# Results of six experts stored as long rows, with the tokens laid out to match

## The chip, the cores and the metric

The kernel runs on one core of a Trainium2 chip. The metric is device time in microseconds of one execution. Below, PE is TensorE (matrix products), DVE is VectorE, ACT is ScalarE, POOL is GpSimd and SP is SyncE; the last two mostly issue DMAs here.

## The reference

Eight experts each apply a two-layer network to their own 256 tokens: a product with w1, a bias, a ReLU, a product with w2 and a second bias.

```python
n_experts, capacity, hidden, expert_hidden = 8, 256, 512, 2048
# x [8, 256, 512], w1 [8, 512, 2048], w2 [8, 2048, 512], b1 [8, 2048], b2 [8, 512], all float32

def reference(x, w1, w2, b1, b2):
    h = np.matmul(x, w1) + b1[:, np.newaxis, :]
    h = np.maximum(h, 0)
    return (np.matmul(h, w2) + b2[:, np.newaxis, :]).astype(np.float32)
```

The weights are 67 MB in float32, x and the result 4.2 MB each.

## The kernel before

Weights are loaded by DMAs from GpSimd that turn float32 into float16 on the way. Each of the two weight pools has three buffers. Names: P = 128 partitions, nTB = 2 blocks of 128 tokens in an expert, nKC = 4 chunks of the hidden size, nJ = 16 chunks of the expert's hidden size, B = 32, LAG = 3.

The tokens come first. x of experts 0 and 1 is loaded as float32 by SyncE and cast by VectorE, two tokens to a partition; experts 2 and 3 share one load, four tokens to a partition; experts 4 to 7 share another, eight to a partition. The first product needs x with the hidden size on the partitions, so VectorE transposes blocks of 32 by 32. The order in which tokens stand in `xT` is free: whatever it is, the result comes out in that order. The code picks it so that partition p of the result's block tb holds token 2p + tb.

```python
    def transposes(e):
        t, p0, R = x16[e]              # R tokens to a partition
        n = R // nTB                   # 1, 2 or 4
        xT[e] = xT_pool.tile([P, nKC, T], fp16, tag="xT", name="xT")      # two buffers
        for g in range(T // R // B):
            src = t[p0 + B * g : p0 + B * (g + 1)]
            for b in range(nB):
                block = src[:, :, b * (H // nB) : (b + 1) * (H // nB)].rearrange(
                    "p (n tb) (i kc) -> p tb kc n i", tb=nTB, kc=nKC)
                out = xT[e][b * B : (b + 1) * B].rearrange(
                    "p kc (tb g i n) -> p tb g kc n i", tb=nTB, i=B, n=n)
                if n == 1:
                    nc.vector.transpose(out=out[:, :, g, :, 0, :], in_=block[:, :, :, 0, :])
                    continue
                for tb in range(nTB):
                    nc.vector.transpose(out=out[:, tb, g], in_=block[:, tb])
```

The first product adds b1 in the ReLU of ScalarE. b1 is brought on to the partitions by four transposes (`b1T`) on VectorE; in the order of the instructions they stand after the 16 transposes of expert 0 and the first seven of expert 1.

```python
    def first_product(e):
        for j in range(nJ):
            ph = psum_h.tile([P, T], fp32, ...)                           # three buffers
            for kc in range(nKC):
                matmul(out=ph, lhsT=w1_sb[e][...j...], rhs=xT[e][:, kc, :], ...)
            nc.scalar.activation(out=hT[e][:, j, :], in_=ph, func=Relu, bias=b1T[...], scale=1.0)
            if j == nJ // 2 and e + 1 < E:
                transposes(e + 1)
```

The second product leaves two blocks in PSUM, `po[0]` and `po[1]`. VectorE and ScalarE copy one each to SBUF, and the result is stored in rows of two tokens (4 KB). The stores of experts 0 to 5 are held back until every weight load is issued.

```python
    LATE = range(E - 2)
    PARTS = {E - 2: ((0, 25, False), (25, 121, True), (121, 128, False))}

    def flush(e):
        dst, src = pending.pop(e)
        ordered(nc.gpsimd.dma_start(out=dst, in_=src))

    def store(e, po):
        out_sb = out_pool.tile([P, nTB, H], fp32, tag="out", name="out")
        nc.vector.tensor_copy(out=out_sb[:, 0, :], in_=po[0])
        nc.scalar.copy(out=out_sb[:, 1, :], in_=po[1])
        dst = out[e].rearrange("(p tb) h -> p tb h", tb=nTB)
        if e in LATE:
            pending[e] = (dst, out_sb)
            return
        for p0, p1, scalar in PARTS.get(e, ((0, P, False),)):
            (nc.scalar if scalar else nc.sync).dma_start(out=dst[p0:p1], in_=out_sb[p0:p1])
    # ... (cut)
    ring.append((E + LAG - 3, load_w2, (E - 1, ((0, nJ // 2), (nJ // 2, nJ)))))
    for e in LATE:
        ring.append((e + LAG + 1, flush, (e,)))

    for s in range(E + LAG):
        while ring and ring[0][0] <= s:          # in the order of the list
            _, put, args = ring.pop(0)
            put(*args)
        if s < E:
            first_product(s)
        if s >= LAG:
            second_product(s - LAG)
```

Of the kernel before, what the change touches and what calls it, by code (L numbers as in the profile page):

```python
# [10 lines left out]
def kernel(  # L11
# [9 lines left out]
    nc = tc.nc  # L21
    fp32 = mybir.dt.float32
    fp16 = mybir.dt.float16
    E, T, H = x.shape
    M = w1.shape[2]
    P = 128
    nTB = T // P
    nKC = H // P
    nJ = M // P
    B = 32  # L30
    nB = P // B
    LAG = 3

    LATE = range(E - 2)


    PARTS = {E - 2: ((0, 25, False), (25, 121, True), (121, 128, False))}
# [3 lines left out]
    def ordered(ins):  # L43
        return tc.keep_in_program_order(ins)
# [4 lines left out]
    x_pool = ctx.enter_context(tc.tile_pool(name="xp", bufs=1))  # L49
    xT_pool = ctx.enter_context(tc.tile_pool(name="xTp", bufs=2))  # L50
    hT_pool = ctx.enter_context(tc.tile_pool(name="hT", bufs=LAG + 1))
    out_pool = ctx.enter_context(tc.tile_pool(name="outp", bufs=E))
    psum_h = ctx.enter_context(tc.tile_pool(name="psum_h", bufs=3, space=bass.MemoryType.PSUM))
    psum_o = ctx.enter_context(tc.tile_pool(name="psum_o", bufs=2, space=bass.MemoryType.PSUM))

# [6 lines left out]
    xT = [None] * E  # L62
    w1_sb = [None] * E
    w2_sb = [None] * E
    hT = [None] * E
    pending = {}

    def load_x(first, n):

        R = n * T // P  # L70
        t = x_pool.tile([P, R, H], fp16, tag=f"x{first}", name=f"x{first}")
        ordered(nc.gpsimd.dma_start(  # L72
            out=t, in_=x[first : first + n].rearrange("e (p r) h -> (e p) r h", r=R)
        ))
        for i in range(n):
            x16[first + i] = (t, i * (P // n), R)
# [13 lines left out]
    def transposes(e):  # L90


        t, p0, R = x16[e]
        n = R // nTB
        xT[e] = xT_pool.tile([P, nKC, T], fp16, tag="xT", name="xT")
        for g in range(T // R // B):
            src = t[p0 + B * g : p0 + B * (g + 1)]
            for b in range(nB):
                block = src[:, :, b * (H // nB) : (b + 1) * (H // nB)].rearrange(
                    "p (n tb) (i kc) -> p tb kc n i", tb=nTB, kc=nKC)  # L100
                out = xT[e][b * B : (b + 1) * B].rearrange(
                    "p kc (tb g i n) -> p tb g kc n i", tb=nTB, i=B, n=n)
                if n == 1:
                    nc.vector.transpose(out=out[:, :, g, :, 0, :], in_=block[:, :, :, 0, :])  # L104
                    continue
                for tb in range(nTB):
                    nc.vector.transpose(out=out[:, tb, g], in_=block[:, tb])  # L107

    def first_product(e):
        hT[e] = hT_pool.tile([P, nJ, T], fp16, tag="hT", name="hT")  # L110
        for j in range(nJ):
            bias_at = j * B + e * nB + nB - 1
            ph = psum_h.tile([P, T], fp32, tag="ph", name="ph")
            for kc in range(nKC):
                ordered(nc.tensor.matmul(  # L115
                    out=ph,
                    lhsT=w1_sb[e][:, kc, :].rearrange("p (q j) -> p q j", j=nJ)[:, :, j],
                    rhs=xT[e][:, kc, :],
                    start=(kc == 0),
                    stop=(kc == nKC - 1),  # L120
                ))
            nc.scalar.activation(  # L122
                out=hT[e][:, j, :],
                in_=ph,
                func=mybir.ActivationFunctionType.Relu,
                bias=b1T[:, bias_at : bias_at + 1],
                scale=1.0,
            )
            if j == nJ // 2 and e + 1 < E:
                transposes(e + 1)  # L130

    def flush(e):
        dst, src = pending.pop(e)
        ordered(nc.gpsimd.dma_start(out=dst, in_=src))  # L134

    def store(e, po):
        out_sb = out_pool.tile([P, nTB, H], fp32, tag="out", name="out")
        nc.vector.tensor_copy(out=out_sb[:, 0, :], in_=po[0])  # L138
        nc.scalar.copy(out=out_sb[:, 1, :], in_=po[1])  # L139
        dst = out[e].rearrange("(p tb) h -> p tb h", tb=nTB)  # L140
        if e in LATE:
            pending[e] = (dst, out_sb)
            return
        for p0, p1, scalar in PARTS.get(e, ((0, P, False),)):
            (nc.scalar if scalar else nc.sync).dma_start(out=dst[p0:p1], in_=out_sb[p0:p1])

    def second_product(e):
        po = []
        for tb in range(nTB):
            t = psum_o.tile([P, H], fp32, tag=f"po{tb}", name=f"po{tb}")  # L150
            po.append(t)
            ordered(nc.tensor.matmul(  # L152
                out=t, lhsT=ones1, rhs=b2_sb[0:1, e * H : (e + 1) * H], start=True, stop=False,
            ))
        half = nJ // 2 if e == E - 1 else nJ
        for lo in range(0, nJ, half):
            for tb in range(nTB):
                for j in range(lo, lo + half):
                    ordered(nc.tensor.matmul(  # L159
                        out=po[tb],  # L160
                        lhsT=hT[e][:, j, tb * P : (tb + 1) * P],
                        rhs=w2_sb[e][:, j, :],
                        start=False,
                        stop=(j == nJ - 1),
                    ))
        store(e, po)

    x32 = []
    for e in range(nXF32):
# [4 lines left out]
        out=b2_sb,  # L174
        in_=b2.rearrange("e h -> (e h)").rearrange("(o f) -> o f", o=1),
# [4 lines left out]
    for e in range(nXF32):  # L180
        t = x_pool.tile([P, nTB, H], fp16, tag=f"x{e}", name=f"x{e}")
        nc.vector.tensor_copy(out=t, in_=x32[e])  # L182
        x16[e] = (t, 0, nTB)
        if e == 0:
            transposes(e)


    for b in range(nB):
        nc.vector.transpose(  # L189
            out=b1T[b * B : (b + 1) * B, nB - 1 - b : nB - 1 - b + nJ * B],  # L190
            in_=b1_rows.rearrange("r (i j) -> r j i", j=nJ),
# [4 lines left out]
    ring = []  # L196
# [5 lines left out]
        if s >= LAG:  # L202
            ring.append((s - 2, load_w2, (s - LAG,)))
    ring.append((E + LAG - 3, load_w2, (E - 1, ((0, nJ // 2), (nJ // 2, nJ)))))
    for e in LATE:
        ring.append((e + LAG + 1, flush, (e,)))

    for s in range(E + LAG):
        while ring and ring[0][0] <= s:
# [37 lines left out]
```

## Time and profile before

| what | value |
|---|---|
| time, median of 3 runs | 182.44 us (182.09 to 182.93) |
| span of the profiled execution | 180.0 us |
| mean granted TensorE clock | 0.938 |
| DMA queue q0 (issued by GpSimd) | 96.5% of 16 engines' span |
| TensorE busy | 130.3 us (72%) |
| VectorE busy | 78.1 us (43%) |
| ScalarE busy | 62.5 us (35%) |

The span runs from the first to the last instruction of the program; the time is a little longer than that. The page's rows of digits cut the span into 40 slices of 4.5 us; a digit gives the busy share in tenths. GB/s counts the bytes of the packets as written, and a weight is written at half the bytes that it is read at. In lists of instructions, the number after x is a count, and what stands behind `<-` in brackets is what ended the engine's idle time.

### The profile page before, as it was taken

Reading aid. Unit: us, or ns where it says so; the run is one execution under the profiler, and the core shown is the slowest. Engines: PE = TensorE matmul, PEld = TensorE weight load, DVE = VectorE, ACT = ScalarE, POOL = GpSimd, SP = SyncE. Lnnn points to the kernel's source line nnn. Section 1 sums busy time; section 2 is a strip of 40 time slices with the busy share of each in tenths; the row PEclk is TensorE's granted clock in tenths of the full one; section 3 lists DMA queues with packets and bytes.
Section 4 is the critical chain, followed back from the end, with each engine's and each line's share of the span. In section 5 each row is a group of like instructions: output and inputs, shape, how many; then the busy total and the mean of one; then the engine's idle time right before and its main releaser. Section 6 shows DMA issues by size and latency. Waiting matters only on the chain.

```text
span 180.0 us, 1937 instructions
## 1 busy us (share of the span) xinstructions
PE 130.3 (72%) x784; PEld 87.4 (49%) x784; DVE 78.1 (43%) x111; ACT 62.5 (35%) x137; POOL 15.0 (8%) x31
## 2 busy tenths in 40 slices
PE   0006199999398950899769994959796899959960
PEld 0004079998286410794359543934395343324420
DVE  1999931988000099999990697000000010101010
ACT  0000558999177010491137403930186001100110
POOL 7100000220201010001100001000100008010000
PEclk9999999999879996599988999987999699999998
DMA  6999999998999999899999999999998999899996
GB/s 207 259 226 198 233 200 208 233 231 182 231 229 193 218 233 226 186 229 229 211 200 233 226 193 222 229 215 197 233 229 189 222 229 226 186 215 209 330 421 246
DMA packets 4260, 40.56 MB, mean 225 GB/s; under 512 B 508, under 2 KB 524, under 8 KB 1948
## 3 DMA queue, kind: packets, MB, share of 16 engines
q0 software_dynamic: 3664, 38.35, 96.5%
q1 hardware_dynamic: 476, 1.70, 2.6%
q10 hardware_dynamic: 112, 0.39, 0.5%
q8 instruction: 6, 0.10, 0.2%
q14 instruction: 2, 0.02, 0.0%
HBM read 71.39 MB, written 4.19 MB: 420 GB/s over the span
## 4 chain that ended last, share of the span: by engine, by line
DMA 44%; PE 30%; another core or an unknown queue 11%; DVE 9%; ACT 1%; issue 1%; POOL 0%; POOLq 0%; ACTq 0%
DMA w1sb<-in_w_dram 26%; PE ph L115 18%; DMA w2sb<-in_w_dram 17%; PE po L159 12%; DVE xT L104 6%; DVE b1T L189 2%; DMA x<-in_x_dram 2%; DVE x L182 1%; ACT L122 1%; PE po L152 1%; ACT out L139 0%; POOL w2sb L88 0%; ACT hT L122 0%; POOLq L88 0%
## 5 line engine op out<-in xcount | busy, mean ns | idle before, releaser
L115 PE MATMUL ph<-xT,w1sb 128*128 128x256 f16 x512 | 66.4, 298 | 36.2 <-DMA w1sb<-in_w_dram 24.9
L115 PEld LDWEIGHTS <-w1sb 128*128 128x128 f16 x512 | 60.9, 148 | 42.5 <-DMA w1sb<-in_w_dram 34.3
L107 DVE STREAM_TRANSPOSE xT<-x 32x256 f16<-32x256 f16 (+1 forms) x64 | 53.0, 888 | 31.9 <-DMA x<-in_x_dram 18.2
L159 PE MATMUL po<-w2sb,hT 128*128 128x512 f16 x256 | 59.7, 393 | 7.6 <-DMA w2sb<-in_w_dram 7.5
L122 ACT ACTIVATE hT<-ph,b1T 128x256 f16<-128x256 f32 x128 | 56.5, 474 | 24.6 <-PE ph L115 24.5
L159 PEld LDWEIGHTS <-hT 128*128 128x128 f16 x256 | 25.6, 100 | 41.6 <-issue 14.9
L138 DVE COPY out<-po 128x512 f32<-128x512 f32 x8 | 5.5, 692 | 58.3 <-PE po L159 58.2
L139 ACT COPY out<-po 128x512 f32<-128x512 f32 x8 | 4.7, 586 | 67.3 <-PE po L159 67.3
L104 DVE STREAM_TRANSPOSE xT<-x 32x256 f16<-32x256 f16 x32 | 13.9, 436 | 0.5
L88 POOL DMA_DIRECT2D w2sb<-in_w_dram x9 | 4.8, 532 | 73.3 <-PE po L159 73.3
L80 POOL DMA_DIRECT2D w1sb<-in_w_dram x8 | 4.9, 609 | 64.7 <-PE ph L115 63.9
L122 ACT ACT_TABLE_LOAD x1 | 1.3, 1283 | 20.2 <-DVE b1T L189 20.2
L152 PE MATMUL po<-b_sb,ones 1*128 1x512 f16 x16 | 4.8, 379 | 0.0
L189 DVE STREAM_TRANSPOSE b1T<-b_rows 32x512 f32<-32x512 f32 x4 | 4.1, 1037 | 0.1
L134 POOL DMA_DIRECT2D out_dram<-out x6 | 3.2, 536 | 7.2 <-DMA w2sb<-in_w_dram 7.2
L182 DVE CAST x<-x 128x1024 f16<-128x1024 f32 x2 | 1.4, 693 | 3.2 <-DMA x<-in_x_dram 3.2
L152 PEld LDWEIGHTS <-ones 1*128 1x128 f16 x16 | 0.9, 92 | 2.1 <-issue 2.1
L72 POOL DMA_DIRECT2D x<-in_x_dram x2 | 1.1, 554 | 0.0
L178 DVE MEMSET ones<- 1x128 f16 x1 | 0.2, 165 | 0.8 <-PEq L231 0.8
L177 POOL DMA_DIRECT2D b_rows<-in_b_dram x1 | 0.5, 515 | 0.0
L173 POOL DMA_DIRECT2D b_sb<-in_b_dram x1 | 0.5, 511 | 0.0
L231 POOL MEMSET const-float32-0.0<- 128x1 f32 x1 | 0.1, 99 | 0.2 <-issue 0.2
(3 smaller groups left out, 0.3 us busy)
## 6 DMA issues: line engine op xcount, KB each, us to landing
w1sb<-in_w_dram POOLq DMA_DIRECT2D x8, 2048.0 KB, 33.6
w2sb<-in_w_dram POOLq DMA_DIRECT2D x7, 2048.0 KB, 43.2
out_dram<-out POOLq DMA_DIRECT2D x6, 512.0 KB, 22.7
w2sb<-in_w_dram POOLq DMA_DIRECT2D x2, 1024.0 KB, 17.4
x<-in_x_dram SPq DMA_DIRECT2D x2, 512.0 KB, 3.8
x<-in_x_dram POOLq DMA_DIRECT2D x1, 1024.0 KB, 30.3
x<-in_x_dram POOLq DMA_DIRECT2D x1, 512.0 KB, 24.0
out_dram<-out SPq DMA_DIRECT2D x1, 512.0 KB, 4.4
```

The costliest lines, as they stand in the source:

```text
L80: ordered(nc.gpsimd.dma_start(out=w1_sb[e], in_=w1[e].rearrange("(p kc) m -> p kc m", kc=nKC)))
L88: ordered(nc.gpsimd.dma_start(out=w2_sb[e][:, lo:hi], in_=src[:, lo:hi]))
L104: nc.vector.transpose(out=out[:, :, g, :, 0, :], in_=block[:, :, :, 0, :])
L107: nc.vector.transpose(out=out[:, tb, g], in_=block[:, tb])
L115: ordered(nc.tensor.matmul(out=ph, lhsT=w1_sb[e][:, kc, :].rearrange("p (q j) -> p q j", j=nJ)[:, :, j], rhs=xT[e][:, kc, :], start=(kc == 0),
L122: nc.scalar.activation(out=hT[e][:, j, :], in_=ph, func=mybir.ActivationFunctionType.Relu, bias=b1T[:, bias_at : bias_at + 1], scale=1.0,)
L134: ordered(nc.gpsimd.dma_start(out=dst, in_=src))
L138: nc.vector.tensor_copy(out=out_sb[:, 0, :], in_=po[0])
L139: nc.scalar.copy(out=out_sb[:, 1, :], in_=po[1])
L152: ordered(nc.tensor.matmul(out=t, lhsT=ones1, rhs=b2_sb[0:1, e * H : (e + 1) * H], start=True, stop=False,))
L159: ordered(nc.tensor.matmul(out=po[tb], lhsT=hT[e][:, j, tb * P : (tb + 1) * P], rhs=w2_sb[e][:, j, :], start=False, stop=(j == nJ - 1),))
L189: nc.vector.transpose(out=b1T[b * B : (b + 1) * B, nB - 1 - b : nB - 1 - b + nJ * B], in_=b1_rows.rearrange("r (i j) -> r j i", j=nJ),)
```

## The change

The results of experts 0 to 5 no longer take one tile each. Experts 0 to 3 share a tile of 128 partitions, experts 4 and 5 one of 64: 32 partitions for an expert, and eight consecutive tokens (16 KB) on each. Each tile is stored by one DMA, so that a row of the store is 16 KB long and not 4 KB, and two DMAs take the place of six.

For this, token 8q + 2k + tb has to come out on partition 32k + q of the result's block tb. So the transposes write their columns in another order, and each block of the result is copied in four pieces of 32 partitions to the place it has in the shared tile. Where a block of x holds tokens of several of these quarters (f of them: 4 for experts 0 and 1, 2 for experts 2 and 3, 1 for 4 and 5) the order needs one dimension more, and the transposes of experts 0 and 1 come in twice as many instructions of half the size. Experts 6 and 7 stay as they were.

```diff
-    LATE = range(E - 2)
+    GROUPS = {0: 4, 4: 2}
+    SPLIT = 4
...
+    group_pool = ctx.enter_context(tc.tile_pool(name="groups", bufs=1))
-    out_pool = ctx.enter_context(tc.tile_pool(name="outp", bufs=E))
+    out_pool = ctx.enter_context(tc.tile_pool(name="outp", bufs=2))
...
         n = R // nTB
+        split = SPLIT if e in group_of else 1
+        f = 1 if split == 1 else split // n
+        to = ("p kc (tb g i f n) -> p tb g kc n i f" if split == 1
+              else "p kc (tb f n g i) -> p tb g kc n i f")
...
-                    "p (n tb) (i kc) -> p tb kc n i", tb=nTB, kc=nKC)
-                out = xT[e][b * B : (b + 1) * B].rearrange(
-                    "p kc (tb g i n) -> p tb g kc n i", tb=nTB, i=B, n=n)
-                if n == 1:
-                    nc.vector.transpose(out=out[:, :, g, :, 0, :], in_=block[:, :, :, 0, :])
+                    "p (n tb) (i f kc) -> p tb kc n i f", tb=nTB, kc=nKC, f=f)
+                out = xT[e][b * B : (b + 1) * B].rearrange(to, tb=nTB, i=B // f, f=f, n=n)
+                if n == 1 and f == 1:
+                    nc.vector.transpose(out=out[:, :, g, :, 0, :, 0], in_=block[:, :, :, 0, :, 0])
                     continue
...
-        out_sb = out_pool.tile([P, nTB, H], fp32, tag="out", name="out")
-        nc.vector.tensor_copy(out=out_sb[:, 0, :], in_=po[0])
-        nc.scalar.copy(out=out_sb[:, 1, :], in_=po[1])
-        dst = out[e].rearrange("(p tb) h -> p tb h", tb=nTB)
-        if e in LATE:
-            pending[e] = (dst, out_sb)
+        if e in group_of:
+            first, n = group_of[e]
+            split, rows = SPLIT, P // SPLIT
+            if e == first:
+                results[e] = group_pool.tile(
+                    [n * rows, split * nTB, H], fp32, tag=f"out{e}", name=f"out{e}")
+        else:
+            first, n, split, rows = e, 1, 1, P
+            results[e] = out_pool.tile([P, nTB, H], fp32, tag="out", name="out")
+        out_sb = results[first]
+        at = (e - first) * rows
+        for k in range(split):
+            part = slice(k * rows, (k + 1) * rows)
+            nc.vector.tensor_copy(out=out_sb[at : at + rows, k * nTB, :], in_=po[0][part])
+            nc.scalar.copy(out=out_sb[at : at + rows, k * nTB + 1, :], in_=po[1][part])
+        dst = out[first : first + n].rearrange("e (p r) h -> (e p) r h", r=split * nTB)
+        if e in group_of:
+            if e == first + n - 1:
+                pending[first] = (dst, out_sb)
             return
...
-    for e in LATE:
-        ring.append((e + LAG + 1, flush, (e,)))
+    for first, n in GROUPS.items():
+        ring.append((first + n + LAG, flush, (first,)))
```

More of the change, by code (lines that the diff above doesn't have):

```diff
@@ L66 @@
     pending = {}
+    results = {}
+    group_of = {first + i: (first, n) for first, n in GROUPS.items() for i in range(n)}
     def load_x(first, n):
@@ L130, in first_product, with flush @@
                 transposes(e + 1)
-    def flush(e):
-        dst, src = pending.pop(e)
+    def flush(first):
+        dst, src = pending.pop(first)
         ordered(nc.gpsimd.dma_start(out=dst, in_=src))
     def store(e, po):
-        out_sb = out_pool.tile([P, nTB, H], fp32, tag="out", name="out")
-        nc.vector.tensor_copy(out=out_sb[:, 0, :], in_=po[0])
-        nc.scalar.copy(out=out_sb[:, 1, :], in_=po[1])
-        dst = out[e].rearrange("(p tb) h -> p tb h", tb=nTB)
-        if e in LATE:
-            pending[e] = (dst, out_sb)
+        if e in group_of:
[17 more added lines that the diff above has]
+                pending[first] = (dst, out_sb)
             return
```

## The prediction

> **What bounds the kernel now.** I read the page's top first: the queue table and the three rows in tenths of the span.
>
> ```profile
> span 180.0 us, 1937 instructions
> PE 130.3 (72%) x784; PEld 87.4 (49%) x784; DVE 78.1 (43%) x111; ACT 62.5 (35%) x137; POOL 15.0 (8%) x31
> ...
> DMA  6999999998999999899999999999998999899996
> ...
> q0 software_dynamic: 3664, 38.35, 96.5%
> ...
> HBM read 71.39 MB, written 4.19 MB: 420 GB/s over the span
> ```
>
> No engine is busy for three quarters of the span, while GpSimd's DMA queue (q0) fills 96.5% of the 16 DMA engines' time. The DMA row has a low digit only in the first and the last slice. So the kernel is a stream of transfers, and two things can change its time: a stretch in which the stream has nothing to do, or packets that move their bytes at another rate.
>
> Next, the landings, asked of the weight loads one at a time. w1 of expert 2 is issued at 4.0 us and lands 33.1 us later, at 37.1; w1 of expert 3 is issued at 31.1 and lands 16.8 later, at 47.9; w2 of expert 0 at 58.1. One load of 4.19 MB takes 9.7 us wherever only weights flow, which is 432 GB/s. The important spot is the reload at 31 us, which the GpSimd timeline shows:
>
> ```profile
> 4.00 0.97 POOL L80 DMA_DIRECT2D w1sb<-in_w_dram  x1
> 31.08 0.53 POOL L80 DMA_DIRECT2D w1sb<-in_w_dram  x1 [26.11 <-PE ph L115]
> ```
>
> For 26 us nothing is issued; the queue lives on what was issued by 4 us, and that is used up at 37.1. The reload waits for TensorE's last read of expert 0's w1. It comes 6.0 us before the queue runs dry: that is all the slack there is. What TensorE waits for at this point is in the timeline of VectorE for the same stretch:
>
> ```profile
> 4.16 0.69 DVE L182 CAST x<-x 128x1024 f16<-128x1024 f32 x1 [3.17 <-DMA x<-in_x_dram]
> 4.88 7.18 DVE L104 STREAM_TRANSPOSE xT<-x 32x256 f16<-32x256 f16 x16
> 12.10 0.69 DVE L182 CAST x<-x 128x1024 f16<-128x1024 f32 x1
> 12.82 3.12 DVE L104 STREAM_TRANSPOSE xT<-x 32x256 f16<-32x256 f16 x7
> 15.96 4.19 DVE L189 STREAM_TRANSPOSE b1T<-b_rows 32x512 f32<-32x512 f32 x4
> ```
>
> VectorE works without a pause from 4.9 to 20.16 us, and only then is b1T there, for which the first ReLU waits ("ACT L122 <- DVE b1T L189: 20.2" in the view of waits). TensorE fills its three PSUM buffers and stands until 22.05. From there expert 0 takes to 30.8, and the reload follows at 31.1. So **any microsecond that VectorE loses before 20 us moves the reload**.
>
> Last, the end. The timeline shows TensorE without a gap from 159.39, when expert 6's w2 has landed, to 174.0; the last store is issued at 174.6 and lands 4.4 us later. The windows there have these columns: length, the five engines' busy time (count), clock, DMA share, GB/s.
>
> ```profile
> 150.00:152.00 2.00, 2.00 (x11) 0.87 (x9) 0.00 (x0) 0.00 (x0) 2.00 (x5) 1.00 1.19 254
> ...
> 170.00:172.00 2.00, 2.00 (x11) 0.93 (x10) 0.00 (x0) 0.00 (x0) 0.00 (x0) 1.00 1.01 414
> 172.00:174.00 2.00, 2.00 (x10) 0.68 (x7) 0.69 (x1) 0.00 (x0) 0.00 (x0) 1.00 1.05 426
> 174.00:176.00 2.00, 0.00 (x1) 0.00 (x0) 0.00 (x0) 0.59 (x1) 0.00 (x0) 1.00 1.01 412
> 176.00:178.00 2.00, 0.00 (x0) 0.00 (x0) 0.00 (x0) 0.00 (x0) 0.00 (x0) 1.00 0.96 391
> ```
>
> After 168 us only stores flow, and at full share. Weights count 4 bytes read and 2 written, so their 216 GB/s is 432 of reading; the stores' 410 or so is 95% of that already.
>
> [...]
> - [...] The second store after the change has 64 partitions. No run so far has such a transfer of size.
> - [...] of 32x512 transposes, those of experts 4 to 7 write every fourth element (8 bytes apart) and take 1328 ns, where the rate of the contiguous ones would give about 700.
> [...]
> - [...] between 170 and 172 us, q0 and the two other queues' packets alternate.
>
> **The change part by part.**
> 1. *The stores.* Removed: six stores of 128 rows of 4 KB, 48 packets per DMA engine. Added: two of 16 KB rows, 128 and 64 of them, 12 packets per engine. In the packet records a 4096-byte store packet takes 159 ns; a weight packet that reads 16 KB takes 625. If a 16 KB store packet takes as long as that, 4 x 159 = 636 becomes 625 or a little less: 12 x 11 = 0.13 us, with the marker packets (9 ns each) some 0.2 us. The bytes are the same and the engines were full. So the gain that the change is for is **0.2 us**, 0.1% of the time.
> 2. *Where they sit.* They still stand behind all loads in the queue, and start to move at about 168. Only the 64-partition store can differ[...]. I give that an even chance.
> 3. *Copies from PSUM.* Each expert's two copies become four on 32 partitions each. Duration follows the 512 elements per partition: VectorE 4 x 692 = 2.8 us, ScalarE 4 x 586 = 2.3 us per expert, +2.1 and +1.8. They fall at 81 to 160 us, where both engines are idle more than half the time and TensorE waits on weights. Worth 0 on the path.
> 4. *Transposes of experts 4 and 5.* Written contiguously now: 16 x (1328 - 700) = 10 us of VectorE saved, off the path. 0.
> 5. *Transposes of experts 0 and 1.* 16 instructions of 256 elements become 32 of 128 each, which write in the order "i f": neighbouring elements 64 bytes apart. This lies in the critical start: all 32 of expert 0 and 7 of expert 1 come before b1T. [...] With 13 ns between instructions, expert 0 takes 10.0, 15.1 or 24.4 us instead of 7.2; the seven take 2.2, 3.3 or 5.3 instead of 3.1. b1T is late by 1.9, 8.1 or 19.4 us.
> 6. *What that does to the stream.* The reload moves from 31.1 to 33.0, 39.2 or 50.5. Packets begin about 1.5 us after an issue (SyncE's first: issued 0.74, packet at 1.77[...]). The queue is dry at 37.1. Gap: none, 3.6 or 14.9 us. After it the queue is tens of microseconds deep (a load issued at 45.0 lands 46.5 later), so a gap is neither made up nor repeated. Experts 2 and 3, whose 16 transposes write 128 bytes apart, take 12 us each instead of 6.5 and delay TensorE, but weights wait for it there, not the other way round.
>
> Sum for the middle rate: 182.44 - 0.2 + 3.6 = 185.8[...].
>
> **Rivals.**
> - *The strided write is free, the stream never starves.* For it: elements 4 bytes apart cost nothing (448 ns against 436). Against: 8 bytes nearly double. Then -0.2 for the stores[...]: 182.2 to 184.3. 30%.
> - *Main line[...].* 185.8[...]. 45%.
> - [...] The gap is 15 us: 197 to 199; experts 2 and 3 then take 21 us each on VectorE, and the backlog is nearly used up later too. 25%.
> - *Long rows help more than packets tell.* TensorE ends at 174.0 and a lone 0.5 MB store needs some 3.4 us (the first x load took that), so the end cannot come before about 178.0: at most 1.2 us better, 181.2. Under 5%.
>
> **Range and chances.** The middle of these is at about 186.6. The low end, 181.9, is the free write with a small gain; the high end, 199[...]. More than 2% faster (below 178.8) is shut out by TensorE's end: 0.02. Above 186.1 fall the costly case (0.25) and somewhat over half of the middle one: 0.53 in all. The rest, 0.45, is within 2%.
>
> **What would show it.** The mean of the 32x128 transposes (298, 460 or 750 ns); the end of b1T (22, 28 or 39 us); the reload's issue (33, 39 or 50 us); a slice around 40 us where the DMA row falls under 8; w1 of expert 3 landing at 47.9 plus the gap. [...] I am wrong if b1T comes before 23 us, if the gap at 40 is there but made up later, or if the stores' last 10 us shrink by more than half a microsecond.

## The result, and the profile after

| | before | after |
|---|---|---|
| time, median | 182.26 us (182.04 to 182.93) | 202.67 us (202.14 to 203.35) |
| ratio | | 1.1117 (95% interval 1.1089 to 1.1145) |
| span of the profiled execution | 180.0 us | 200.4 us |
| mean granted TensorE clock | 0.938 | 0.932 |

The changed kernel takes 20.4 us more, above the stated range. The page's top shows where to look: q0 fell from 96.5% to 88.3% of the span, with the same 38.35 MB, and VectorE's busy time rose from 78 to 135 us. In the two rows of digits, each digit is one slice of 5 us.

```profile
span 200.4 us, 1997 instructions
...
DVE  2999999999999999999278069939913200450010
...
DMA  8999999208999999999999999999999997299994
...
q0 software_dynamic: 3024, 38.35, 88.3%
```

The transposes by shape, first before and then after, are those of experts 0 and 1, of 2 and 3, and of 4 to 7; behind the first bar stand their busy time in us and the mean of one in ns:

```profile
L104 DVE STREAM_TRANSPOSE xT<-x 32x256 f16<-32x256 f16 x32 | 13.9, 436 | 0.5
L107 DVE STREAM_TRANSPOSE xT<-x 32x256 f16<-32x256 f16 x32 | 12.8, 448 | 7.3 <-PE ph L115 7.1
L107 DVE STREAM_TRANSPOSE xT<-x 32x512 f16<-32x512 f16 x32 | 40.1, 1328 | 24.7 <-DMA x<-in_x_dram 18.2 <-PE ph L115 6.1
...
L114 DVE STREAM_TRANSPOSE xT<-x 32x128 f16<-32x128 f16 x64 | 41.2, 814 | 0.5
L114 DVE STREAM_TRANSPOSE xT<-x 32x256 f16<-32x256 f16 x32 | 39.9, 1431 | 0.2
L114 DVE STREAM_TRANSPOSE xT<-x 32x512 f16<-32x512 f16 x32 | 30.7, 1007 | 15.1 <-PE ph L122 14.8
```

The DMA row has two holes, near 40 us and near 170 us, and VectorE shows no pause from its first transpose to 95 us. VectorE's timeline, to set against the one of before:

```profile
4.80 20.67 DVE L114 STREAM_TRANSPOSE xT<-x 32x128 f16<-32x128 f16 x32
25.50 0.69 DVE L202 CAST x<-x 128x1024 f16<-128x1024 f32 x1
26.23 4.65 DVE L114 STREAM_TRANSPOSE xT<-x 32x128 f16<-32x128 f16 x7
30.89 4.13 DVE L209 STREAM_TRANSPOSE b1T<-b_rows 32x512 f32<-32x512 f32 x4
34.95 61.63 DVE L114 STREAM_TRANSPOSE xT<-x 32x128 f16<-32x128 f16 x65
```

Expert 0's transposes take 20.7 us instead of 7.2, so b1T ends at 35.0 us instead of 20.2. The last line merges three shapes; it runs on through experts 1 to 4. GpSimd's reload of w1, which sets how soon the stream of weights goes on, follows TensorE:

```profile
45.01 0.53 POOL L84 DMA_DIRECT2D w1sb<-in_w_dram  x1 [40.13 <-PE ph L122]
```

and the DMA engines stand still meanwhile. The last two columns of these windows are the DMA share and GB/s:

```profile
36.00:38.00 2.00, 1.07 (x6) 0.87 (x6) 1.99 (x4) 1.61 (x5) 0.00 (x0) 1.00 0.01 0
38.00:40.00 2.00, 2.00 (x11) 1.58 (x10) 1.97 (x5) 1.24 (x3) 0.00 (x0) 1.00 0.00 0
...
44.00:46.00 2.00, 0.71 (x7) 0.47 (x5) 1.99 (x4) 1.23 (x3) 0.99 (x2) 1.00 0.00 0
46.00:48.00 2.00, 0.00 (x0) 0.00 (x0) 1.97 (x5) 0.00 (x0) 0.59 (x2) 0.95 1.00 139
```

In the packet records q0's last packet ends at 37.1 us and the next begins at 46.3: 9.2 us of nothing. The second hole is of another kind. The chain of work that ended last has changed its owner. These are its shares of the span, before and then after:

```profile
DMA 44%; PE 30%; another core or an unknown queue 11%; DVE 9%; ACT 1%; issue 1%; POOL 0%; POOLq 0%; ACTq 0%
```

```profile
PE 46%; DVE 42%; ACT 6%; issue 2%; DMA 2%
```

After the change no weight stands in this chain: its 2% of DMA is the first load of x, and in the view of waits TensorE waits for a weight only once, for the first one ("PEld L122 <- DMA w1sb<-in_w_dram: 15.2, 1, 15.2", where PEld is TensorE loading a weight). VectorE works from 4.8 us to the last transpose of expert 3 at 91.35, and the first product of expert 3 begins at 91.48. From there on the chain holds only TensorE and ScalarE. This is one turn of it, without the short pieces that the view calls issue:

```profile
101.16 7.03 PE po L179 x32
108.21 0.45 ACT out L158
108.80 0.58 ACT out L158
109.39 0.58 ACT out L158
109.97 0.59 ACT out L158
110.58 0.48 ACT hT L129
111.11 5.84 PE ph L122 x52
```

The second product of expert 0 ends, ScalarE makes its four copies, and only then comes the ReLU that frees a PSUM buffer for the first product of expert 4. The timeline puts TensorE's idle time there at 1.62 us:

```profile
108.01 1.47 PE L122 MATMUL ph<-xT,w1sb 128*128 128x256 f16 x12
111.11 5.84 PE L122 MATMUL ph<-xT,w1sb 128*128 128x256 f16 x52 [1.62 <-ACT hT L129]
```

Four such turns stand in the chain (experts 4 to 7). TensorE is now so late that weights wait for it: w2 of expert 6 has landed at 170.1 us, the load for expert 7 is issued at 173.7, and between 170 and 174 us the DMA share is 0.00. TensorE ends at 196.1 us instead of 174.0. The span is the sum of three stretches: 91.5 us until expert 3's product begins, 104.6 us of TensorE, 4.3 us for the last copy and store. The 9.2 us in which the stream stands still delay the weights, but no instruction of this chain waits for them.

### The profile page after: what moved, and what is told of

Read it like the earlier page. It is cut to its first block, busy times and chain, and to the rows that moved or that the text cites. A ratio compares the mean times of both kernels' runs of the same rounds, so it can differ in the third digit from the quotient of the medians.

```text
span 200.4 us, 1997 instructions
## 1 busy us (share of the span) xinstructions
PE 126.3 (63%) x784; PEld 86.2 (43%) x784; DVE 135.2 (67%) x161; ACT 72.3 (36%) x155; POOL 12.9 (6%) x27
## 3 DMA queue, kind: packets, MB, share of 16 engines
q0 software_dynamic: 3024, 38.35, 88.3%
## 4 chain that ended last, share of the span: by engine, by line
PE 46%; DVE 42%; ACT 6%; issue 2%; DMA 2%
DVE xT L114 39%; PE po L179 28%; PE ph L122 16%; ACT out L158 5%; PE po L172 2%; DVE b1T L209 2%; DMA x<-in_x_dram 2%; ACT hT L129 1%; DVE x L202 1%
## 5 line engine op out<-in xcount | busy, mean ns | idle before, releaser
L114 DVE STREAM_TRANSPOSE xT<-x 32x128 f16<-32x128 f16 (+2 forms) x128 | 111.7, 1017 | 15.8 <-PE ph L122 14.8
L122 PE MATMUL ph<-xT,w1sb 128*128 128x256 f16 x512 | 66.6, 296 | 69.8 <-DVE xT L114 54.6
L122 PEld LDWEIGHTS <-w1sb 128*128 128x128 f16 x512 | 60.9, 147 | 75.6 <-issue 55.8
L179 PE MATMUL po<-w2sb,hT 128*128 128x512 f16 x256 | 56.6, 379 | 0.0
L157 DVE COPY out<-po 32x512 f32<-32x512 f32 (+1 forms) x26 | 17.9, 687 | 40.1 <-PE po L179 39.9
L179 PEld LDWEIGHTS <-hT 128*128 128x128 f16 x256 | 24.4, 98 | 31.7 <-issue 3.4
L158 ACT COPY out<-po 32x512 f32<-32x512 f32 (+1 forms) x26 | 15.0, 578 | 52.9 <-PE po L179 52.7
L141 POOL DMA_DIRECT2D out_dram<-out x2 | 1.1, 546 | 8.3 <-ACT out L158 8.3
## 6 DMA issues: line engine op xcount, KB each, us to landing
x<-in_x_dram POOLq DMA_DIRECT2D x1, 1024.0 KB, 26.8
```

Of the source, the lines that this page charges most:

```text
L122: ordered(nc.tensor.matmul(out=ph, lhsT=w1_sb[e][:, kc, :].rearrange("p (q j) -> p q j", j=nJ)[:, :, j], rhs=xT[e][:, kc, :], start=(kc == 0),
L157: nc.vector.tensor_copy(out=out_sb[at : at + rows, k * nTB, :], in_=po[0][part])
L158: nc.scalar.copy(out=out_sb[at : at + rows, k * nTB + 1, :], in_=po[1][part])
L179: ordered(nc.tensor.matmul(out=po[tb], lhsT=hT[e][:, j, tb * P : (tb + 1) * P], rhs=w2_sb[e][:, j, :], start=False, stop=(j == nJ - 1),))
```

## The experiments

**Theory T**: the new order of columns makes VectorE write float16 elements far apart, which slows the transposes; this delays b1T, the reload and the stream. **Rival S**: the long-row stores and the four-part copies cost the time. **Rival N**: it is the doubled number of transposes and not the step between written elements. Each run was timed beside the kernel before on the same chip, and its ratio has a 95% interval; the run on write steps has only a profile. T1, T2 and T3 are versions of Theory T, told with the two runs in which they are tested.

### The transposes alone

```diff
# the changed kernel, but copies, stores and flush of the kernel before
-            nc.vector.tensor_copy(out=out_sb[at : at + rows, k * nTB, :], in_=po[0][part])
-            nc.scalar.copy(out=out_sb[at : at + rows, k * nTB + 1, :], in_=po[1][part])
+        nc.vector.tensor_copy(out=out_sb[:, 0, :], in_=po[0])
+        nc.scalar.copy(out=out_sb[:, 1, :], in_=po[1])
```

> The kernel before with the new order of columns in the transposes of experts 0 to 5; copies and stores as before (so the tokens of the result stand in another order). Theory T (strided writes of the transposes cost the time): nearly all of the loss is here. b1T ends near 35 us, the reload of w1 is issued near 45 us, VectorE transposes without a break until about 91 us, and from there TensorE is followed to the end; the four-part copies on ScalarE, which stood in that chain for about 4 x 1.6 us in the changed kernel, are gone, so about 195 to 197 us. Theory S (the long-row stores and the four-part copies cost the time): 182 to 184 us.

Measured: 195.54 us, ratio 1.0716 (1.0689 to 1.0744). Reload at 44.6 us; VectorE transposes from 34.9 to 96.6 without a pause. With one copy instead of four, ScalarE no longer holds TensorE up: the 64 products of expert 4 run through in 7.15 us, where the changed kernel needs 8.9 with the wait. Both kernels begin expert 3's product at 91.5 us; from there TensorE needs 97.1 us here and 104.6 in the changed kernel.

So 13.2 of the 20.4 us come with the transposes and nothing else changed.

### The copies and stores alone

```diff
# the changed kernel
-        split = SPLIT if e in group_of else 1
+        split = 1                  # in transposes only
```

> The changed kernel with the transposes of the kernel before; four-part copies and the two long-row stores stay (so the tokens of the result stand in another order). Theory T: the stream is never dry, reload at 31 us; the end differs only by the stores: 16 KB packets of 611 ns (a gain of 0.3 us in all)[...]: 182 to 184.5 us. Theory S: 195 us or more.

Measured: 184.28 us, ratio 1.0098 (1.0066 to 1.0131): 2.0 us. Reload at 30.1 us, no hole. Rival S as the main cause falls. The parts add up to 15.2 us, not to 20.4: something happens only when both are there.

### Twice as many transposes, written without steps

```diff
# the kernel before
                 if n == 1:
-                    nc.vector.transpose(out=out[:, :, g, :, 0, :], in_=block[:, :, :, 0, :])
+                    for tb in range(nTB):
+                        nc.vector.transpose(out=out[:, tb, g, :, 0, :], in_=block[:, tb, :, 0, :])
```

> The kernel before with each transpose of experts 0 and 1 made as two of 128 elements instead of one of 256, columns in the old order. Theory T: a 128-element transpose with contiguous writes takes about 300 ns, b1T ends near 22 us, the reload comes near 33 us, still before the queue is dry: 182 to 183 us. Rival N (what costs is the doubled number of instructions, not the step between written elements): 640 ns each as in the changed kernel, b1T at 35 us, reload at 45 us, a gap of 8 us: 190 us or more.

Measured: 182.45 us, ratio 1.0005 (0.9992 to 1.0019). VectorE in this run:

```profile
4.91 8.14 DVE L105 STREAM_TRANSPOSE xT<-x 32x128 f16<-32x128 f16 x32
13.09 0.69 DVE L183 CAST x<-x 128x1024 f16<-128x1024 f32 x1
13.82 1.83 DVE L105 STREAM_TRANSPOSE xT<-x 32x128 f16<-32x128 f16 x7
```

32 of them take 8.1 us (254 ns each, back to back), not 20.7: the same instructions as in the changed kernel but for the order of writing. Rival N falls. (The pattern of writing also has one dimension more in the changed kernel; the next run has none more, and its steps cost as much.)

### The step between written elements, by itself

```python
# no experts' work: one block, read as in the kernel, written `step` elements apart
for step, name in steps.items():                       # 1, 2, 4, 8, 16, 32, 64
    # ... (cut: t, a tile for each step)
    dst = t[0:32, : 256 * step].rearrange(
        "p (tb kc i s) -> p tb kc i s", tb=2, kc=4, s=step)[:, :, :, :, 0]
    for rep in range(8):
        nc.vector.transpose(out=dst[:, rep % 2], in_=src[:, rep % 2])     # 128 elements
    for rep in range(8):
        nc.vector.transpose(out=dst, in_=src)                             # 256 elements
```

> Not the experts' work: only VectorE transposes of 32 x 128 and 32 x 256 float16 elements, read 4 elements apart as in the kernel, written 1, 2, 4, 8, 16, 32 or 64 elements apart. Lines of 16 bytes: about 300 ns for 128 elements at steps 1 and 2, 460 at step 4, and 640 to 750 from step 8 on, no further growth. Words of 8 bytes: 460 from step 4 on, no further growth, so that the 640 ns of the changed kernel would need another cause. Lines of 64 bytes: growth up to step 32.[...]

The tiles are named by the step, and the mean of one instruction in ns stands after the busy time:

```profile
L40 DVE STREAM_TRANSPOSE sixtyfour<-x 32x256 f16<-32x256 f16 x8 | 10.4, 1305 | 0.3
L40 DVE STREAM_TRANSPOSE eight<-x 32x256 f16<-32x256 f16 x8 | 10.4, 1299 | 0.3
...
L40 DVE STREAM_TRANSPOSE sixteen<-x 32x256 f16<-32x256 f16 x8 | 9.9, 1232 | 0.3
L40 DVE STREAM_TRANSPOSE four<-x 32x256 f16<-32x256 f16 x8 | 5.9, 732 | 0.3
...
L40 DVE STREAM_TRANSPOSE two<-x 32x256 f16<-32x256 f16 x8 | 3.6, 453 | 0.3
...
L40 DVE STREAM_TRANSPOSE one<-x 32x256 f16<-32x256 f16 x8 | 3.5, 432 | 0.3
```

Up to a step of 2 next to nothing changes, step 4 takes 732 ns, step 8 takes 1299, and beyond that nothing grows. A cost for each stretch of 16 bytes that an instruction writes to (a line, for short) fits this; it is an estimate from these means. Steps 8, 4 and 2 touch 256, 128 and 64 lines, and from 128 to 256 lines the time grows by 567 ns, 4.43 ns a line. What is left over is 165 ns; 64 lines then give 449 ns, and 453 are measured. The 32 lines of step 1 would give 307 ns; 432 are measured, so something else sets the time there. The 128-element instructions show the same growth (their recorded durations overlap, so that 8 of them back to back are taken: 4.6 us in all at step 32, 1.7 at step 1). That is 575 ns for one at step 32; in the changed kernel the pace is 646, and no run explains the rest. There the written elements are 64 bytes apart in runs of four and not throughout.

### Only the start, only the middle

```diff
# the changed kernel, start only
-        split = SPLIT if e in group_of else 1
+        split = SPLIT if e in group_of and e not in (2, 3) else 1
# the changed kernel, middle only
-        split = SPLIT if e in group_of else 1
+        split = SPLIT if e in group_of and e >= 2 else 1
```

> The changed kernel with the new column order in the transposes of experts 0, 1, 4 and 5 alone; experts 2 and 3 are transposed as before (their tokens stand in another order). Theory T1 (the late start alone sets the loss): as in the changed kernel, reload at 45 us and first landing after it at 57.3 instead of 47.9, and the queue never dry again, so 182.3 + 9.4 + 2.0 for the stores = 193.7 us. Theory T2 (the late start is a part, and only together with the slow transposes of experts 2 and 3, which keep TensorE waiting until 91.5 us, does TensorE's own work become the end): also 193.7 here, so 9 us less than the changed kernel. Theory T3 (only the stretch of VectorE counts): about 187.

> The changed kernel with the new column order in the transposes of experts 2 to 5 alone; experts 0 and 1 are transposed as before (their tokens stand in another order). Reload at 31 us, no gap. VectorE is through with expert 3 near 72 us. Theory T1 or T2: TensorE then needs the 104.6 us that it took from this point on in the changed kernel, so it ends at 176 at most, which is no later than the weights allow: 184 to 185.5 us (184.3 being the stores' part). Theory T3: 195 us.

Measured: the start only, 194.92 us, ratio 1.0706 (1.0676 to 1.0735); the middle only, 183.9 us, ratio 1.0086 (1.0068 to 1.0104). Both have the 2.0 us of the stores in them, so the start costs 10.6 us and the middle, by itself, nothing. The start only is 1.2 us above what T1 and T2 expected (193.7), far from the 187 of T3. In the second run VectorE is busy with experts 2 and 3 until 75.5 us and TensorE waits 24.4 us for it in the view of waits, yet q0 never runs dry. From 70.4 us on TensorE sets the pace there too, with the same waits of 1.63 us for ScalarE's copies, and it ends at 175.0 us, where it ends at 175.5 with the stores alone: the middle uses up all the room that there was. T3 falls. In the first run TensorE catches up: TensorE's timeline there has these lines, with the wait in brackets:

```profile
85.93 5.84 PE L122 MATMUL ph<-xT,w1sb 128*128 128x256 f16 x52 [1.63 <-ACT hT L129]
...
101.91 8.77 PE L122 MATMUL ph<-xT,w1sb 128*128 128x256 f16 x64 [2.60 <-DMA w1sb<-in_w_dram]
```

At 86 us it is still late and waits for ScalarE's copies, at 102 it waits for weights again. In the changed kernel expert 3's product begins at 91.5 us, 21.1 later than with the middle only, and TensorE ends at 196.1, again 21.1 later: nothing is left to hide a delay in, and the last weights wait for TensorE. T1, by which the late start alone sets the loss, falls; T2 stands: start and middle together cost 7.8 us more (202.67 - 194.92) than the start.

### One store of 128 partitions

```diff
# the run with copies and stores alone
-    GROUPS = {0: 4, 4: 2}
+    GROUPS = {0: 4}
+    LATE = (4, 5)              # copied whole, 4 KB rows, as in the kernel before
```

> Old transposes; only experts 0 to 3 share a tile and a store of 128 rows of 16 KB; experts 4 and 5 are copied whole and stored in 4 KB rows over 128 partitions as before (tokens of experts 0 to 3 in another order). If the 2.0 us of the run with all the stores are the 64-partition store[...]: 182.0 to 182.6 us. If they come from the four-part copies or from packets of 16 KB standing before the last stores: 183.5 to 184.3 us.

Measured: 181.75 us, ratio 0.9974 (0.9966 to 0.9981). So the 2.0 us belong to the store of 64 partitions. The run also takes the four-part copies from experts 4 and 5, but TensorE ends at about the same time in both (175.5 us with both stores, 175.7 here), and the difference lies behind its end: 6.1 us against 4.2. What is left, long rows and four-part copies, is a gain of 0.46 us. The windows at the end, first of the run with both stores, then of this one:

```profile
174.00:176.00 2.00, 1.49 (x7) 0.49 (x5) 0.49 (x1) 0.47 (x1) 0.00 (x0) 1.00 0.98 328
176.00:178.00 2.00, 0.00 (x0) 0.00 (x0) 0.00 (x0) 0.11 (x1) 0.00 (x0) 1.00 0.91 287
```

```profile
174.00:176.00 2.00, 1.67 (x8) 0.58 (x6) 0.67 (x1) 0.29 (x1) 0.00 (x0) 1.00 1.01 410
176.00:178.00 2.00, 0.00 (x0) 0.00 (x0) 0.00 (x0) 0.29 (x1) 0.00 (x0) 1.00 0.82 334
```

With the 64-partition store the engines are as busy (0.98 and 1.01) and move 328 instead of 410 GB/s. In the packet records of the first run its 64 packets of 16 KB take 812 ns on average beside others, those of the 128-partition store 616.

### Eight tokens to a partition already when x is loaded

```diff
# the changed kernel
-    for e in range(nXF32):
-        nc.sync.dma_start(out=x32[e], in_=x[e].rearrange("(p tb) h -> p tb h", tb=nTB))
+    for e in range(nXF32):     # and experts 2 and 3 by GpSimd to partitions 32.. and 96..
+        nc.sync.dma_start(out=x32[64 * e : 64 * e + 32], in_=x[e].rearrange("(p r) h -> p r h", r=8))
```

> The changed kernel's result and stores, right order of tokens, but x of experts 0 to 3 is loaded eight tokens to a partition, as that of 4 and 5 is, so that the columns can be written without steps. A 32x512 transpose with contiguous writes takes 0.67 us, an expert 5.4 us. x needs a cast of 4096 elements per partition for each of experts 0 and 1 (about 2.8 us). b1T near 20 us, reload near 31 us. If the step of the writes is the whole cause of the loss at the start and in the middle: 182.3 + 2.0 for the stores = 184.3 us (183.5 to 185). If the layout costs in another way: 190 us or more.

Measured: 185.01 us, ratio 1.0163 (1.0132 to 1.0194). The transposes of an expert take 5.2 us and the stream has no hole, so of the 20.4 us all but 2.8 are gone. It is 0.7 above the 184.28 of the stores alone, and at the upper end of what was expected. The loads to 32 partitions were slow too: their 16 KB packets took 1172 ns on average, where those of a load to all 128 partitions (in the next run) took 723. x of experts 0 and 1 lands at 5.3 and 7.6 us instead of 4.1 and 5.4, and w1 of expert 0 behind it at 16.8 instead of 15.2; that delay of 1.6 us is still there at 49.5 against 47.9.

### One load of x for experts 0 to 3

```diff
# experts 0 to 3 in one tile and store, 4 and 5 in LATE as above
+    nc.sync.dma_start(out=x32, in_=x[0:4].rearrange("e (p r) h -> (e p) r h", r=8))
+    nc.vector.tensor_copy(out=t, in_=x32)
```

> The right order of tokens, and both costs taken away: x of experts 0 to 3 comes in one load of 128 partitions, eight tokens to a partition, and is cast in one instruction of 4096 elements per partition (2.28 us for 32 partitions, and no longer for 128), so that all columns of these experts are written without steps; their results share one tile and one store of 128 rows of 16 KB; experts 4 and 5 are stored in 4 KB rows over 128 partitions as before. x lands at about 7 us, b1T near 22 us (b1 stands behind w1 of expert 0, which starts 1.2 us later), reload near 33 us, before the queue is dry at 37. Theory: the time of the run with this store alone, 181.8 us (181.4 to 182.3), a little under the kernel before. If the later start still moves the stream: 183 to 184 us.

Measured: 182.83 us, ratio 1.0019 (1.0002 to 1.0036). A miss by 1 us. The cast took 2.29 us for the 128 partitions, where it took 2.28 for 32 in the run before this one. The later start goes with it: x is four times as long, takes turns with w1 on the DMA engines and lands at 13.4 us instead of the expected 7. b1T ends at 25.2, the reload is issued at 35.8, and the first w1 after it lands at 48.9, 1.0 us later than in the kernel before.

### Experts 2 to 5 instead of 0 to 3

```diff
# the changed kernel
-    GROUPS = {0: 4, 4: 2}
-    X_LOADS = {2: 2, 4: 4}
+    GROUPS = {2: 4}
+    LATE = (0, 1)              # copied whole, 4 KB rows, as in the kernel before
+    X_LOADS = {2: 4, 6: 2}
```

> The right order of tokens. The shared tile holds experts 2 to 5 instead of 0 to 3: x of these four comes in one GpSimd load of 128 partitions, eight tokens to a partition (that of 6 and 7 in a later one, four to a partition), so all their columns are written without steps, and the start of experts 0 and 1 stays as in the kernel before. Results of 2 to 5 go out in one store of 128 rows of 16 KB, those of 0 and 1 in 4 KB rows as before. b1T at 20 us, reload at 31, and the queue is dry 2.4 us later than before, since 1 MB more stands in it. Theory: no cost is left and the gain of the long rows (0.46 us in the run with that store alone) remains: 181.8 us (181.4 to 182.2), ratio 0.996 to 0.999. If the gain came from something else in that run: 182.3 us.

Measured: 181.82 us, ratio 0.997 (0.9958 to 0.9983), as much as the run with the one long-row store gained. VectorE's start is that of the kernel before, and the experts with long rows are transposed in 5.2 us each:

```profile
15.94 4.19 DVE L213 STREAM_TRANSPOSE b1T<-b_rows 32x512 f32<-32x512 f32 x4
20.16 4.04 DVE L112 STREAM_TRANSPOSE xT<-x 32x256 f16<-32x256 f16 x9
29.98 5.23 DVE L115 STREAM_TRANSPOSE xT<-x 32x512 f16<-32x512 f16 x8 [5.78 <-DMA x<-in_x_dram]
```

This is 20.9 us faster than the changed kernel and 0.3% faster than the kernel before.

## Why the prediction was wrong, point by point

- **The bound.** Right for the kernel before, and for what moves the reload: VectorE before b1T, with 6 us of slack. Measured: b1T late by 14.9 us, the reload by 13.9, the queue dry for 9.2. Wrong for the kernel after: its time is set by VectorE up to 91.5 us and by TensorE from there, not by the stream.
- **Step 5, the transposes of experts 0 and 1: the step that failed first.** The text had three estimates for one of these transposes, 298, 460 and 750 ns, and leaned on the middle one (45%), giving 185.8. They were the author's; no trace had shown such a transpose. The middle one takes the growth at 8 bytes between elements, which the trace before has, for the most that a step can cost. The run on write steps shows that it is not: 732 ns at step 4, 1299 at step 8, a growth that fits about 4.4 ns for each 16-byte line; step 4 only looked like an upper limit because two elements share a line there. That is nearest to the third estimate (25%), which let the cost grow further. It was right in kind and somewhat high: 750 ns per transpose were expected, but 20.67 / 32 = 646 is the pace back to back (the recorded mean is 814, because the records overlap). Hence b1T at 35 us, not 39, and the reload at 45, not 50.5. The trace before could not decide: elements 4 bytes apart took 448 ns against 436, 8 apart 1328 for 512. A cost that stops growing at 8 bytes and one that grows up to 16 fit both equally. In the run on write steps two elements to a line took 732 ns and four took 453, 21 more than step 1.
- **Step 6, the stream after the gap: the step that puts the time outside the range.** With the measured gap of 9.2 us in place of 3.6 the text's own sum gives 191.4 us, or 193.4 with the 2.0 us measured for the stores; 202.67 were measured. The rest is not in the stream. The text took the slow transposes of experts 2 and 3 as free, because "weights wait for it there, not the other way round": landed weights wait for TensorE. They do, but TensorE's own work can then become the end. With the middle alone it just fails to (183.9 us). After a late start TensorE begins expert 3 at 91.5 us, needs 104.6 us from there to its last product, and that is then the end. Nor is the gap never repeated: TensorE now frees the buffers so late that the queue runs dry a second time, from 169.8 to 175.0 us. Start and middle together cost 7.8 us more than the start, which is why the time lies above even the costly rival's 197 to 199. That rival saw it coming ("the backlog is nearly used up later too") and did not put a number on it; that its number comes near to the measured one is luck, since its gap of 14.9 us was too long.
- **The gap's size.** Packets began 1.24 us after the reload's issue (45.01 to 46.25); 1.5 had been estimated.
- **Step 3, the copies: "worth 0 on the path".** True where weights set the pace: the run with one long-row store has them for four experts and is faster. A copy of 32 partitions took about as long as one of 128: 686 ns against 692 on VectorE, 578 against 585 on ScalarE. In the changed kernel the copies cost TensorE 1.62 us in each of four turns, 6.5 us. The run with the transposes alone, which has no such waits, is 7.1 us faster.
- **Step 1, the stores' gain.** Expected 0.2 us from both stores; the run with one of them gained 0.46 (0.35 to 0.62 by the interval). A 16 KB packet took 611 ns where four of 4 KB take 636; eight of them on each DMA engine make 8 x 25 ns = 0.2 us. Where the rest comes from, no run shows.
- **Step 2, the 64 partitions.** The even chance came out as a cost: 2.0 us in the run with copies and stores alone, and gone in the run with 128 partitions, which makes it 2.3 us by the difference of the ratios (1.0098 - 0.9974) x 182.3. In these two runs the store from 64 partitions was the slower one, with 812 ns a packet against 616 and 328 GB/s against 410 in the windows from 174 to 176 us. Why a single packet takes longer, no run here shows. In the changed kernel this store is not the end: its last packet ends at 195.6 us, before TensorE at 196.1.
- **Step 4.** Right: experts 4 and 5 were transposed faster, off the path. The 700 ns for a 32x512 transpose written without steps were the author's estimate; in the changed kernel five in a row took 3.32 us, 664 ns each.
- **The chances.** "Slower" had the largest share, 0.53, but the range ended at 199.

## What to carry to other kernels

A layout chosen for a transfer can cost more where the data is rearranged than it gains; for transposes like these, count the 16-byte lines that each instruction writes (about 4.4 ns each beyond 64 of them, by the estimate from the run on write steps) before the transfer's gain is counted. When a stream of loads is the bound, look for the one point where the queue runs low, and ask what the engines before it may still lose; and check whether a delay that is hidden by itself still is so behind another one: the slow transposes of experts 2 and 3 cost nothing alone, and after the late start they set the end. If the order can be had from the load (rows of the same length in and out, on all 128 partitions), as for experts 2 to 5 here, the rearranging costs no more than before: 5.2 us for an expert, where experts 2 and 3 took 6.5 in the kernel before.

## What the runs showed of the hardware

- VectorE's 32x32 transpose of 256 float16 elements took 432 and 453 ns when written in steps of 1 and 2 elements, 732 in steps of 4, and 1232 to 1305 in steps of 8 to 64.
- SBUF to HBM in rows of 16 KB took 611 ns a packet, 26.8 GB/s per DMA engine; in rows of 4 KB 159 ns, 25.8. A store from 64 partitions was slower: its 64 packets took 812 ns on average in the run with copies and stores alone and 837 in the changed kernel, where the 17 that began between 193 and 194 us, with few other packets beside them, took 1295.
- Two queues took turns on a DMA engine packet by packet, so that the shorter packets got the smaller share. In the run with one load of x, 81 of its 128 packets had begun by 5.8 us; the other 47 came in three rounds 1.8 us apart, 0.62 us each, with weight packets of 1.23 us between them, and x landed 12.7 us after its issue.
